# Weight-quarter sums by accumulating transfers, and another order of the seven products, in the up-projection of a decoder layer

## The chip, the cores and the metric

The kernel runs on one core of one Trainium2 chip. Its engines are TensorE (PE; its weight loads are listed apart, as PEld), VectorE (DVE), ScalarE (ACT), GpSimd (POOL) and SyncE (SP). SP and POOL do little here but issue transfers, each from a queue in which one transfer waits behind the one before it. The metric is the device time of one execution in microseconds (us), the median of several runs.

## The reference

One decoder layer on 576 tokens (512 of a prompt and 8 x 8 of samples), width 2048, everything in f32. Cut to the part that the change touches, the ConvFFN:

```python
up = rmsnorm(x, g_ffn) @ w_up                    # 2048 -> 2 * 5632
up_ext = jnp.concatenate([ffn_hist.astype(up.dtype), up], axis=1)
upc = causal_dwconv(up_ext, w_dw_f, b_dw_f)      # width 3
x = x + (jax.nn.silu(upc[..., :D_FF]) * upc[..., D_FF:]) @ w_down
```

Ahead of it stand the input projection, two head groups and the output projection; behind it a gate for a per-layer input and a last norm. Outputs are the activations and the new convolution states.

## The kernel before

**Phases.** All products of weights run one after the other on TensorE, as phases of one stream: mix (input projection), out and out2 (output projection), proj (per-layer input), **up**, down0 to down3, ple, tail. The tokens lie along the free axis as two halves of 288.

**Weights.** They come from DRAM as one stream, `in_wstream`, in the order in which they are used. A *unit* is 8 tiles of 128 x 128, 512 KB, and is loaded on SP's queue into a buffer `raw` (5 buffers, L189 in the function that loads a unit). Half a unit, 4 tiles, is a *piece*. To keep f32 accuracy each piece is split in two: ScalarE copies it to a rounded high half `wh` (L229) and VectorE subtracts that to get the low half `wl` (L230). Each has 4 buffers, so a piece can be split once TensorE has finished with the piece four before it. Activations are split in the same way, and a tile takes three matmuls: high by high, high by low, low by high (L695, L696, L697 in up).

**Up.** It computes 44 pairs `j` of column tiles: tile j and tile 44 + j of `w_up`, which the gate later multiplies. For a pair the weights are a 2 x 2 block of quarters (even and odd row tiles by the two column tiles), the tokens two halves, and one level of Strassen's scheme in Winograd's form takes 7 products of 8 tiles in place of 8. A product is 2 pieces, or 24 matmuls. The tile stream holds the four quarters of a pair as units u to u + 3: q11, q21, q22, q12. Products 1, 2 and 4 use q11, q12 and q22 as they are. The others use sums: product 7 q21 + q11, product 5 q21 + q22, product 6 that plus q11, product 3 that again plus q12, one after the other in two buffers `sum` of half a quarter each. VectorE makes these sums when a piece is prepared (L205, L209, L211). The activation side of each product, `sx`, was made before.

**Results of a product.** A product accumulates in one bank of a PSUM tile of two banks; there are three such tiles. The table `PRODS` sets the order of the products, and `banks` pairs them: in the order 1, 5, 6, 7, 4, 2, 3 the tiles hold (1, 5), (6, 7), (4, 2), and product 3 takes the bank of 6. The output tiles `ua` and `ub` are put together from the banks by one ScalarE copy after product 1 (L706) and VectorE operations after 6 (L709, L710), 7 (L713, L714), 4 (L716), 2 (L718) and 3 (L720). Waits between engines are kept by tile, not by bank: a matmul that begins in the second bank of a tile waits for readers of its first bank.

**Order of work.** A scheduler orders each engine's instructions; it moves a few matmuls of the next product but one ahead, where the next product has to wait. Half of the pairs write `ua` and `ub` to DRAM (L722, L723, POOL) and are fetched later, the other half go on at once to convolution and gate, whose result is written (`hidd`, L726, POOL). This work, and norm work in the first pairs, is dealt out between pieces as a queue `todo`. In the last pair the first fetches for the down phase are issued after products 1 and 6.

**At the start of up** the buffers `sum` of the first two pairs are those of two spare x rows and two spare activation tiles (`SPARE`, taken in turn by even and odd pairs). The proj phase just before it writes 16 results to DRAM from POOL (`pjd`, L885), and the scaled x rows are copied on ScalarE (`xg`, L565).

Of the kernel before, what the change touches and what calls it, by code (L numbers as in the profile page):

```python
# [11 lines left out]
ALU = mybir.AluOpType  # L12
PSUM = bass.MemoryType.PSUM

P = 128
# [4 lines left out]
HT = 288  # L20
# [6 lines left out]
NF = DFF // P  # L27
# [19 lines left out]
HGRP = 6  # L47


PRODS = [1, 5, 6, 7, 4, 2, 3]  # L50

VEC = {}
_n = 0
# [6 lines left out]
UNIT = 8  # L60
SUB = 4
# [66 lines left out]
def weight_order():  # L128

    tiles, pieces = [], []
    for phase, outs, ks in plan():
        n = len(tiles)
        if phase == "up":
            (w, a), (_, b) = outs
            for m, odd in ((a, 0), (b, 0), (b, 1), (a, 1)):
                tiles += [(w, k, m) for k in range(odd, KT, 2)]
            pieces += [(n // UNIT, prod, half) for prod in PRODS for half in range(2)]
        else:  # L140
            tiles += [(w, k, m) for k in ks for w, m in outs]
            for s in range(-(-n // SUB), -(-len(tiles) // SUB)):
                pieces.append((s * SUB // UNIT, s % 2))
    assert len(tiles) % UNIT == 0
    return tiles, pieces
# [3 lines left out]
def trunk_kernel(ctx: ExitStack, tc: tile.TileContext, A, O):  # L149
    nc = tc.nc  # L150
    groups = plan()
    order, pieces = weight_order()
    n_w = len(order)
# [5 lines left out]
    def tl(shape, tag, name, bufs=1, dt=F32):  # L159
        return pool.tile(shape, dt, tag=tag, name=name, bufs=bufs)  # L160

    def tmp(name, shape=(P, 2, HT)):
        return tl(list(shape), "t", name, bufs=6)


    raws, parts = {}, {}
# [7 lines left out]
    SPARE = [f"xh{LATE[2]}", f"xl{LATE[2]}", f"res{KT - 2}", f"res{KT - 1}"]  # L174
# [6 lines left out]
    def load_unit(u):  # L181
        if u in raws or u * UNIT >= n_w:
            return
        t = tl([P, UNIT * P], "raw", f"raw{u}", bufs=5)
        if u == 0:
            nc.sync.dma_start(t[:, : SUB * P], A["wstream"][u][:, : SUB * P])
            nc.sync.dma_start(t[:, SUB * P :], A["wstream"][u][:, SUB * P :])
        else:
            nc.sync.dma_start(t, A["wstream"][u])  # L189
        raws[u] = t  # L190

    sums = {}

    def source(p):

        if len(p) == 2:
            u, half = p
            return raws[u][:, half * SUB * P : (half + 1) * SUB * P]
        u, prod, half = p
        q11, q21, q22, q12 = (raws[u + n][:, half * SUB * P : (half + 1) * SUB * P] if u + n in raws else None  # L200
                              for n in range(4))
        if prod in (4, 1, 2):
            return {4: q22, 1: q11, 2: q12}[prod]
        if prod == 7:
            nc.vector.tensor_tensor(out=q21, in0=q21, in1=q11, op=ALU.add)  # L205
            return q21
        if prod == 5:
            sums[half] = tl([P, SUB * P], SPARE[2 * (u // 4 % 2) + half], f"sum{u}_{half}")
            nc.vector.tensor_tensor(out=sums[half], in0=q21, in1=q22, op=ALU.add)  # L209
        else:  # L210
            nc.vector.tensor_tensor(out=sums[half], in0=sums[half], in1=q11 if prod == 6 else q12, op=ALU.add)  # L211
        return sums[half]

    def prepare(s):
        if s in parts or s >= len(pieces):
            return
        p = pieces[s]
        u = p[0] if len(p) == 2 else p[0] + {1: 0, 5: 1, 6: 1, 7: 1, 4: 2, 2: 3, 3: 3}[p[1]]
        for a in range(4):
            load_unit(u + a)  # L220
        spare = s - (len(pieces) - 4)
        if spare < 0:
            h = tl([P, SUB * P], "wh", f"wh{s}", bufs=4, dt=F32R)
            l = tl([P, SUB * P], "wl", f"wl{s}", bufs=4, dt=F32R)
        else:
            h = tl([P, SUB * P], HID[32 + 2 * spare], f"wh{s}", dt=F32R)
            l = tl([P, SUB * P], HID[33 + 2 * spare], f"wl{s}", dt=F32R)
        src = source(p)
        nc.scalar.activation(h, src, AF.Copy)  # L229
        nc.vector.tensor_tensor(out=l, in0=src, in1=h.bitcast(F32), op=ALU.subtract)  # L230
        parts[s] = (h, l)

    at = {"tile": 0}

    def weights(i=None):

        n = at["tile"] if i is None else at["tile"] + i
        s = n // SUB
        for a in range(s, s + (4 if s >= 3 else 2)):
            prepare(a)  # L240
        if i is None:
            at["tile"] += 1
        h, l = parts[s]
        o = n % SUB * P
        return h[:, o : o + P], l[:, o : o + P]
# [117 lines left out]
    def deal():  # L363
        state["credit"] += state["rate"]
        if chain:
            take(chain)
        while (urgent or todo) and state["credit"] > 0:
            take(urgent or todo)
        if not (urgent or todo):
            state["credit"] = min(state["credit"], 0.0)  # L370
# [285 lines left out]
    def slot_of(j):  # L656
        return ORDER.index(j) % (len(HID) // 2)
# [8 lines left out]
    def fetch_hidden(j, slot):  # L666

        if j in hid_d:
            def fetch():
                p = tmp(f"hq{j}")  # L670
                nc.sync.dma_start(p, hid_d[j])
                split_hidden(j, slot, p)

            return [(0.7, fetch)]
        z = {}

        def fetch_up():
            for m, tag in ((j, "cv"), (NF + j, "vn")):
                z[m] = tl([P, 2, HT], tag, f"uz{m}", bufs=2)
                nc.sync.dma_start(z[m], up_d[m])  # L680

        return ([(0.0, fetch_up)] + conv_f(j, j, lambda: z[j]) + conv_f(j, NF + j, lambda: z[NF + j])
                + hidden(j, lambda p: split_hidden(j, slot, p)))

    banks = {}

    def up_pair(j):

        q = {}
        for n, prod in enumerate(PRODS):  # L690
            q[prod] = dst = banks[prod]
            for k in range(KT // 2):
                wh, wl = weights()
                bh, bl = sums_x[k][prod]
                nc.tensor.matmul(dst, wh, bh, start=k == 0, stop=False)  # L695
                nc.tensor.matmul(dst, wh, bl, start=False, stop=False)  # L696
                nc.tensor.matmul(dst, wl, bh, start=False, stop=k == KT // 2 - 1)  # L697
                if k % SUB == SUB - 1:
                    deal()
            if j == NF - 1 and prod in (1, 6):  # L700
                for i in ORDER[: 4] if prod == 1 else ORDER[4 : COMING[0]]:
                    for _, f in fetch_hidden(i, slot_of(i)):
                        f()
            if prod == 1:
                a = tl([P, 2, HT], "cv", f"ua{j}", bufs=2)
                nc.scalar.activation(a[:, 0, :], q[1], AF.Copy)  # L706
            if prod == 6:
                u = tl([P, HT], "q", f"uu{j}", bufs=2)
                nc.vector.tensor_tensor(out=u, in0=q[6], in1=a[:, 0, :], op=ALU.subtract)  # L709
                nc.vector.tensor_tensor(out=a[:, 1, :], in0=q[5], in1=u, op=ALU.add)  # L710
            if prod == 7:
                b = tl([P, 2, HT], "vn", f"ub{j}", bufs=2)
                nc.vector.tensor_tensor(out=u, in0=u, in1=q[7], op=ALU.subtract)  # L713
                nc.vector.tensor_tensor(out=b[:, 1, :], in0=q[5], in1=u, op=ALU.add)  # L714
            if prod == 4:
                nc.vector.tensor_tensor(out=b[:, 0, :], in0=u, in1=q[4], op=ALU.subtract)  # L716
            if prod == 2:
                nc.vector.tensor_tensor(out=a[:, 0, :], in0=q[2], in1=a[:, 0, :], op=ALU.add)  # L718
            if prod == 3:
                nc.vector.tensor_tensor(out=a[:, 1, :], in0=q[3], in1=a[:, 1, :], op=ALU.subtract)  # L720
        if j in up_d:
            nc.gpsimd.dma_start(up_d[j], a)  # L722
            nc.gpsimd.dma_start(up_d[NF + j], b)  # L723
            return
        todo.extend(conv_f(j, j, lambda: a) + conv_f(j, NF + j, lambda: b)
                    + hidden(j, lambda p: nc.gpsimd.dma_start(hid_d[j], p)))  # L726
# [23 lines left out]
    for gi, (phase, outs, ks) in enumerate(groups):  # L750
# [21 lines left out]
        if phase == "up" and prev != "up":  # L772
            settle(lambda: not todo)
            state["credit"], state["rate"] = 0.0, 0.36
            acc6 = [psum.tile([P, 2, 512], F32, tag="acc", name=f"acc_up{n}", bufs=3) for n in range(3)]
            banks.update({p: acc6[n // 2][:, n % 2, :HT] for n, p in enumerate((1, 5, 6, 7, 4, 2))})
            banks[3] = banks[6]
            rows_of(ORDER[0])
        if phase == "down0" and prev == "up":
            settle(lambda: not todo)  # L780
# [18 lines left out]
        if phase == "up":  # L799
            j = outs[0][1]  # L800
# [56 lines left out]
        for n, (w, m) in enumerate(outs):  # L857
# [24 lines left out]
            elif w == "w_ple_proj":  # L882
                a = tmp(f"pa{m}")
# [159 lines left out]
```

## Time and profile before

| what | us |
|---|---|
| median of 3 runs (lowest to highest) | 2480.53 (2479.83 to 2482.52) |
| profiled execution, its own time | 2480.28 |
| its span in the trace | 2478.3 |
| TensorE busy | 2449.2 |
| VectorE busy | 1841.9 |
| ScalarE busy | 1093.3 |
| POOL busy | 92.1 |
| DMA, mean over the span | 119 GB/s |
| the phase up in the trace | 677 to 1696 |

The span is what the trace shows from the first to the last instruction; the time of an execution has some 2 us around it. "Busy" for TensorE counts any time in which a matmul is in flight, so it doesn't tell how closely the matmuls follow each other. In the group lists a row gives line, engine, operation, output <- inputs, shapes and count; behind the first bar the busy time and the mean duration of one in ns; behind the second the idle time of the engine just before such instructions and what ended most of it. In the timeline a row begins with start and duration. In the table by stretches the columns are named where it is shown.

### The profile page before, as it was taken

To read this page: it belongs to the slowest core of one execution; us is meant where nothing else is said; L and a number is where in the kernel's file an instruction comes from. 1 tells how busy PE (TensorE), PEld (TensorE's weight loads), DVE (VectorE), ACT (ScalarE), POOL (GpSimd) and SP (SyncE) were. 2 spreads that over 40 slices of the span, in tenths; PEclk is the share of its full clock that TensorE was granted. 3 is DMA by queue.
4 is the path that set the end of the run, shared out by engine and by line. 5 is a ranking of instruction groups with operands and counts; after the bars stand their busy time and mean duration, and the time that the engine had idled before them with its cause. 6 is when DMAs were issued, how large, how long until landed. Compare 5 with 4: busy or idle time off the path is not lost.

```text
span 2478.3 us, 45398 instructions
## 1 busy us (share of the span) xinstructions
PE 2449.2 (99%) x18200; PEld 2418.2 (98%) x18200; DVE 1841.9 (74%) x3243; ACT 1093.3 (44%) x2028; POOL 92.1 (4%) x175
## 2 busy tenths in 40 slices
PE   9999999999999999999999999999999999999997
PEld 9999999999989999999999999999999999999997
DVE  7877788885998888888988888887549762254545
ACT  6444445433754444444544444445335441243334
POOL 1000000000200000000000000000000000000000
PEclk9999999999999999999999999999999999999998
DMA  6332222332653333333333333348425442222332
GB/s 235 94 83 83 84 88 85 127 107 95 227 184 111 109 115 110 110 126 106 102 123 113 102 118 118 97 152 281 127 89 154 136 126 78 85 86 80 116 100 95
DMA packets 106195, 294.70 MB, mean 119 GB/s; under 512 B 23568, under 2 KB 27792, under 8 KB 105984
## 3 DMA queue, kind: packets, MB, share of 16 engines
q1 hardware_dynamic: 96096, 259.20, 33.5%
q0 software_dynamic: 9744, 32.60, 3.6%
q8 instruction: 142, 2.33, 0.4%
q14 instruction: 69, 0.57, 0.1%
q10 hardware_dynamic: 144, 0.01, 0.0%
HBM read 255.43 MB, written 36.32 MB: 118 GB/s over the span
## 4 chain that ended last, share of the span: by engine, by line
PE 88%; issue 8%; DVE 2%; DMA 1%; ACT 1%; POOL 0%; DVEq 0%; ACTq 0%; SPq 0%; POOLq 0%
PE acc L835 18%; PE acc L839 18%; PE acc L837 18%; PE acc_up L695 10%; PE acc_up L697 10%; PE acc_up L696 10%; DVE wl L230 1%; DMA raw<-in_wstream 0%; PE vps L492 0%; PE mps L530 0%; ACT wh L229 0%; DVE y L945 0%; PE acc L908 0%; PE acc L909 0%; PE acc L910 0%
## 5 line engine op out<-in xcount | busy, mean ns | idle before, releaser
L229 ACT ACTIVATE wh<-raw 128x512 fp32r<-128x512 f32 x792 | 497.3, 632 | 1051.4 <-PE acc L837 670.5
L230 DVE TENSOR_TENSOR wl<-raw,wh 128x512 fp32r<-128x512 f32 x792 | 540.8, 688 | 390.9 <-ACT wh L229 383.3
L695 PE MATMUL acc_up<-sx,wh 128*128 128x288 f32 x2464 | 734.3, 299 | 2.5 <-ACT wh L229 1.2
L697 PE MATMUL acc_up<-sx,wl 128*128 128x288 f32 x2464 | 722.0, 298 | 5.5 <-DVE wl L230 5.1
L696 PE MATMUL acc_up<-sx,wh 128*128 128x288 f32 x2464 | 726.8, 295 | 0.0
L695 PEld LDWEIGHTS acc_up<-sx,wh 128*128 128x128 f32 x2464 | 464.0, 188 | 14.0 <-ACT ua L706 4.7
L697 PEld LDWEIGHTS acc_up<-sx,wl 128*128 128x128 f32 x2464 | 460.5, 188 | 17.5 <-DVE wl L230 17.1
L696 PEld LDWEIGHTS acc_up<-sx,wh 128*128 128x128 f32 x2464 | 464.0, 188 | 0.1
L835 PE MATMUL acc<-xh,wh 128*128 128x288 f32 x1984 | 427.4, 296 | 5.5 <-ACT wh L229 5.3
L839 PE MATMUL acc<-xh,wl 128*128 128x288 f32 x1984 | 423.9, 295 | 0.0
L837 PE MATMUL acc<-xl,wh 128*128 128x288 f32 x1984 | 423.8, 295 | 0.0
L835 PEld LDWEIGHTS acc<-xh,wh 128*128 128x128 f32 x1984 | 318.8, 189 | 7.5 <-ACT wh L229 5.3
L837 PEld LDWEIGHTS acc<-xl,wh 128*128 128x128 f32 x1984 | 319.5, 188 | 0.3 <-issue 0.2
L839 PEld LDWEIGHTS acc<-xh,wl 128*128 128x128 f32 x1984 | 318.4, 188 | 0.3 <-issue 0.3
L839 PE MATMUL acc<-hh,wl 128*128 128x288 f32 x1408 | 300.9, 295 | 0.0
L835 PE MATMUL acc<-hh,wh 128*128 128x288 f32 x1408 | 300.4, 294 | 0.4 <-ACT wh L229 0.4
L837 PE MATMUL acc<-hl,wh 128*128 128x288 f32 x1408 | 300.4, 295 | 0.0
L229 ACT ACTIVATE wh<-sum 128x512 fp32r<-128x512 f32 x264 | 166.5, 631 | 153.2 <-PE acc_up L696 137.3
L835 PEld LDWEIGHTS acc<-hh,wh 128*128 128x128 f32 x1408 | 226.2, 188 | 0.9 <-ACT wh L229 0.6
L837 PEld LDWEIGHTS acc<-hl,wh 128*128 128x128 f32 x1408 | 226.0, 188 | 0.0
L839 PEld LDWEIGHTS acc<-hh,wl 128*128 128x128 f32 x1408 | 225.7, 188 | 0.0
L230 DVE TENSOR_TENSOR wl<-sum,wh 128x512 fp32r<-128x512 f32 x264 | 180.5, 684 | 4.4 <-ACT wh L229 4.0
(191 smaller groups left out, 2146.5 us busy)
## 6 DMA issues: line engine op xcount, KB each, us to landing
raw<-in_wstream SPq DMA_DIRECT2D x395, 512.0 KB
uz<-upd SPq DMA_DIRECT2D x44, 288.0 KB
upd<-ub POOLq DMA_DIRECT2D x22, 288.0 KB, 2.8
upd<-ua POOLq DMA_DIRECT2D x22, 288.0 KB, 2.4
hidd<-hp POOLq DMA_DIRECT2D x22, 288.0 KB, 2.4
hq<-hidd SPq DMA_DIRECT2D x22, 288.0 KB
x<-in_xT SPq DMA_DIRECT2D x16, 288.0 KB
xr<-in_xT SPq DMA_DIRECT2D x16, 288.0 KB
```

Of the source, the lines that this page charges most:

```text
L229: nc.scalar.activation(h, src, AF.Copy)
L230: nc.vector.tensor_tensor(out=l, in0=src, in1=h.bitcast(F32), op=ALU.subtract)
L695: nc.tensor.matmul(dst, wh, bh, start=k == 0, stop=False)
L696: nc.tensor.matmul(dst, wh, bl, start=False, stop=False)
L697: nc.tensor.matmul(dst, wl, bh, start=False, stop=k == KT // 2 - 1)
L835: nc.tensor.matmul(accs[n][:, h, :HT], wh, bh[:, h, :], start=st, stop=False)
L837: nc.tensor.matmul(accs[n][:, h, :HT], wh, bl[:, h, :], start=False, stop=False)
L839: nc.tensor.matmul(accs[n][:, h, :HT], wl, bh[:, h, :], start=False, stop=sp)
```

## The change

The order of the products becomes 5, 7, 1, 6, 4, 2, 3, and the tiles of PSUM hold (5, 7), (1, 6), (4, 2), with product 3 in the bank of 1. The quarters of a pair lie in the stream as q21, q11, q22, q12. VectorE no longer adds weights. When the first unit of a pair is loaded, a new function issues: an accumulating transfer from DRAM onto that raw buffer (q21 + q11, for product 7); for each half, a plain copy of q21 into a `sum` buffer on SP and an accumulating transfer of q22 onto it (for product 5). Once the split of a piece of product 5 has read the sum, an accumulating transfer adds q11 to it, for 6; after 6 another adds q12, for 3. All accumulating transfers are issued by POOL. A pair so has 7 of them and two more plain copies. The function that loads ahead now looks four units ahead from the unit in use. The four VectorE operations that used to be shared between products 6 and 7 all stand behind 6.

```diff
-PRODS = [1, 5, 6, 7, 4, 2, 3]
+PRODS = [5, 7, 1, 6, 4, 2, 3]
...
-            for m, odd in ((a, 0), (b, 0), (b, 1), (a, 1)):
+            for m, odd in ((b, 0), (a, 0), (b, 1), (a, 1)):
...
-        if prod == 7:
-            nc.vector.tensor_tensor(out=q21, in0=q21, in1=q11, op=ALU.add)
-            return q21
-        if prod == 5:
-            sums[half] = tl([P, SUB * P], SPARE[2 * (u // 4 % 2) + half], f"sum{u}_{half}")
-            nc.vector.tensor_tensor(out=sums[half], in0=q21, in1=q22, op=ALU.add)
-        else:
-            nc.vector.tensor_tensor(out=sums[half], in0=sums[half], in1=q11 if prod == 6 else q12, op=ALU.add)
-        return sums[half]
+    def half_of(u, half):
+        return A["wstream"][u][:, half * SUB * P : (half + 1) * SUB * P]
+
+    def load_sums(u):
+
+        nc.gpsimd.dma_start(raws[u], A["wstream"][u + 1], accum_op=ALU.add)
+        for half in range(2):
+            t = sums[u, half] = tl([P, SUB * P], SPARE[2 * (u // 4 % 2) + half], f"sum{u}_{half}")
+            nc.sync.dma_start(t, half_of(u, half))
+            nc.gpsimd.dma_start(t, half_of(u + 2, half), accum_op=ALU.add)
+
+    def load_to(u):
+        for a in range(u, u + 4):
+            if a not in raws and a * UNIT < n_w:
+                load_unit(a)
+                if 0 <= a - first_up < n_up and (a - first_up) % 4 == 0:
+                    load_sums(a)
...
-        u = p[0] if len(p) == 2 else p[0] + {1: 0, 5: 1, 6: 1, 7: 1, 4: 2, 2: 3, 3: 3}[p[1]]
-        for a in range(4):
-            load_unit(u + a)
+        if len(p) == 2:
+            load_to(p[0])
+            src = raws[p[0]][:, p[1] * SUB * P : (p[1] + 1) * SUB * P]
+        else:
+            u, prod, half = p
+            n = {5: 0, 7: 0, 1: 1, 6: 1, 4: 2, 2: 3, 3: 3}[prod]
+            load_to(u + n)
+            src = sums[u, half] if prod in (5, 6, 3) else raws[u + n][:, half * SUB * P : (half + 1) * SUB * P]
...
+        if len(p) == 3 and p[1] in (5, 6):
+            nc.gpsimd.dma_start(src, half_of(u + (1 if prod == 5 else 3), half), accum_op=ALU.add)
...
             if prod == 6:
+                b = tl([P, 2, HT], "vn", f"ub{j}", bufs=2)
                 u = tl([P, HT], "q", f"uu{j}", bufs=2)
                 nc.vector.tensor_tensor(out=u, in0=q[6], in1=a[:, 0, :], op=ALU.subtract)
                 nc.vector.tensor_tensor(out=a[:, 1, :], in0=q[5], in1=u, op=ALU.add)
-            if prod == 7:
-                b = tl([P, 2, HT], "vn", f"ub{j}", bufs=2)
                 nc.vector.tensor_tensor(out=u, in0=u, in1=q[7], op=ALU.subtract)
                 nc.vector.tensor_tensor(out=b[:, 1, :], in0=q[5], in1=u, op=ALU.add)
...
-            banks.update({p: acc6[n // 2][:, n % 2, :HT] for n, p in enumerate((1, 5, 6, 7, 4, 2))})
-            banks[3] = banks[6]
+            banks.update({p: acc6[n // 2][:, n % 2, :HT] for n, p in enumerate((5, 7, 1, 6, 4, 2))})
+            banks[3] = banks[1]
```

In the changed kernel the three matmul lines of up are L702, L703 and L704, the copy after product 1 is L713, the writes of `ua`, `ub` and `hidd` L728, L729 and L732, `pjd` L891; the new transfers are L202 (onto `raw`), L205 (plain copies), L206 (q22 onto `sum`) and L238 (q11 or q12 onto `sum`).

**TensorE inside a pair.** First the kernel before, where product 1 (`sx_2`, tile 7931) ends and product 5 (`sx_3`, second bank of the same tile) is held; the rows between are of product 6 (tile 7932):

```order
L697 MATMUL acc_up_7931<-sx_2_7875,wl_12489 128x288
L695 MATMUL acc_up_7932<-sx_3_7146,wh_12545 128x288 [waits DVE_49,Activation_49]
L696 MATMUL acc_up_7932<-sx_4_7147,wh_12545 128x288
L697 MATMUL acc_up_7932<-sx_3_7146,wl_12546 128x288 [waits DVE_49]
L695 MATMUL acc_up_7932<-sx_3_7271,wh_12545 128x288
L695 MATMUL acc_up_7931<-sx_3_7146,wh_12506 128x288 [waits Activation_49]
L696 MATMUL acc_up_7931<-sx_4_7147,wh_12506 128x288
```

Now the changed kernel, in the order of time: product 5 (tile 7936) goes over to product 7 (`sx_0`, the same tile), and later product 1 (tile 7937) is followed by rows of product 4 (tile 7938) ahead of product 6.

```order
L704 MATMUL acc_up_7936<-sx_3_7885,wl_11979 128x288
L702 MATMUL acc_up_7936<-sx_0_7143,wh_11995 128x288 [waits Activation_49]
L703 MATMUL acc_up_7936<-sx_1_7144,wh_11995 128x288
L704 MATMUL acc_up_7937<-sx_2_7884,wl_12056 128x288
L702 MATMUL acc_up_7938<-sx_0_7143,wh_12107 128x288 [waits Activation_49]
L703 MATMUL acc_up_7938<-sx_1_7144,wh_12107 128x288
L704 MATMUL acc_up_7938<-sx_0_7143,wl_12108 128x288 [waits DVE_49]
L702 MATMUL acc_up_7937<-sx_3_7146,wh_12071 128x288 [waits Activation_49]
```

Between 5 and 7 there are no rows of another product, and the wait of the first row of 7 is that for its own piece; 6 behind 1 stands as 5 behind 1 did, with rows of 4 between instead of rows of 6. Counted over a whole pair, the rows went 1 (24), 6 (8), 5 (24), 6 (16), 4 (6), 7 (24), 4 (18), 3 (9), 2 (24), 3 (15) before, and go 5 and 7 (48), 1 (24), 4 (7), 6 (24), 4 (17), 3 (11), 2 (24), 3 (13) now.

**POOL at the start of up.** Before, the last writes of the proj phase (`pjd`) are followed by the first writes of `ua` and `ub`:

```order
L885 DMA pjd_157<-pa_7884 128x576
L885 DMA pjd_158<-pa_7908 128x576
L885 DMA pjd_159<-pa_7928 128x576
L723 DMA upd_183<-ub_8105 128x576
L722 DMA upd_182<-ua_7982 128x576
```

Now the accumulating transfers of the first pair stand among them (`sum_0` and `sum_1` are the two halves, the row of 128x1024 that of the second pair's raw buffer):

```order
L202 DMA raw_7963<-in_wstream 128x1024 [waits DMAHW5_49,DMAHW0_49,DMAHW6_49,DMASW6_49,DVE_49]
L891 DMA pjd_155<-pa_7835 128x576 [waits DMASW7_49,Activation_49]
L891 DMA pjd_156<-pa_7856 128x576 [waits DMASW0_49,Activation_49]
L206 DMA sum_0_7501<-in_wstream 128x512 [waits DMAHW1_49,DMASW1_49,Activation_49]
L891 DMA pjd_157<-pa_7893 128x576 [waits DMASW2_49,Activation_49]
L206 DMA sum_1_7504<-in_wstream 128x512 [waits DMAHW2_49,DMASW3_49]
L891 DMA pjd_158<-pa_7913 128x576 [waits DMASW4_49,Activation_49]
L891 DMA pjd_159<-pa_7933 128x576 [waits DMASW5_49,Activation_49]
L238 DMA sum_0_7501<-in_wstream 128x512 [waits DMASW6_49,DMASW1_49,DVE_49]
```

The first matmul of up was of product 1, from a plain load, and is now of product 5, from these sums.

**POOL in a steady pair.** Before, the queue holds nothing but three writes for two pairs, here with a neighbour on each side:

```order
L722 DMA upd_198<-ua_11756 128x576 [waits DMASW0_49,DVE_49]
L726 DMA hidd_166<-hp_12483 128x576 [waits DMASW1_49,DVE_49]
L723 DMA upd_201<-ub_12409 128x576 [waits DMASW2_49,DVE_49]
L722 DMA upd_200<-ua_12290 128x576 [waits DMASW3_49,DVE_49]
L726 DMA hidd_167<-hp_13016 128x576 [waits DMASW4_49,DVE_49]
```

Now, for the pair of `sum` 12295 and 12298 and the next one (12568, 12571):

```order
L729 DMA upd_201<-ub_12432 128x576 [waits DMASW4_49,DVE_49]
L202 DMA raw_12565<-in_wstream 128x1024 [waits DMAHW7_49,DMAHW0_49,Activation_49]
L238 DMA sum_0_12295<-in_wstream 128x512 [waits DMASW6_49,DVE_49]
L206 DMA sum_0_12568<-in_wstream 128x512 [waits DMAHW0_49,DMASW7_49,DMASW1_49]
L206 DMA sum_1_12571<-in_wstream 128x512 [waits DMAHW1_49,DMASW2_49]
L238 DMA sum_1_12298<-in_wstream 128x512 [waits DVE_49]
L728 DMA upd_200<-ua_12396 128x576 [waits DVE_49]
L238 DMA sum_0_12295<-in_wstream 128x512 [waits DMASW6_49,DMASW3_49,DVE_49]
L238 DMA sum_1_12298<-in_wstream 128x512 [waits DMASW4_49,DMASW1_49,DVE_49]
```

The queue now holds seven accumulating transfers a pair between the same writes; the sums of the next pair are issued while those of this pair are still in use.

More of the change, by code (lines that the diff above doesn't have):

```diff
@@ L192, in trunk_kernel @@
     sums = {}
[L194 to L203, printed above, removed]
-        if prod == 7:
-            nc.vector.tensor_tensor(out=q21, in0=q21, in1=q11, op=ALU.add)
-            return q21
-        if prod == 5:
-            sums[half] = tl([P, SUB * P], SPARE[2 * (u // 4 % 2) + half], f"sum{u}_{half}")
-            nc.vector.tensor_tensor(out=sums[half], in0=q21, in1=q22, op=ALU.add)
-        else:
-            nc.vector.tensor_tensor(out=sums[half], in0=sums[half], in1=q11 if prod == 6 else q12, op=ALU.add)
-        return sums[half]
+    first_up = min(p[0] for p in pieces if len(p) == 3)
+    n_up = 4 * NF
+    def half_of(u, half):
[12 more added lines that the diff above has]
+                    load_sums(a)
     def prepare(s):
@@ L227, in prepare @@
             l = tl([P, SUB * P], HID[33 + 2 * spare], f"wl{s}", dt=F32R)
-        src = source(p)
         nc.scalar.activation(h, src, AF.Copy)
```

## The prediction

> **What bounds the kernel now.** The first view is the page's list of engines with its chain of waits.
>
> ```profile
> span 2478.3 us, 45398 instructions
> PE 2449.2 (99%) x18200; PEld 2418.2 (98%) x18200; DVE 1841.9 (74%) x3243; ACT 1093.3 (44%) x2028; POOL 92.1 (4%) x175
> PE 88%; issue 8%; DVE 2%; DMA 1%; ACT 1%; POOL 0%; DVEq 0%; ACTq 0%; SPq 0%; POOLq 0%
> ```
>
> TensorE is busy 99% of the span and holds 88% of the chain; VectorE, which the change relieves, holds 2%. A busy TensorE need not be dense, so the second view counts matmuls in stretches of time: the up phase, the down phase behind it, the middle of up, and four shorter pieces at the ends of up.
>
> ```profile
> 677.00:1696.00 1019.00, 1011.09 (x7399) 987.36 (x7398) 867.15 (x1517) 473.21 (x887) 38.77 (x74) 1.00 0.38 122
> 1696.00:2256.00 560.00, 559.57 (x4226) 559.15 (x4225) 328.17 (x531) 216.38 (x445) 3.60 (x9) 1.00 0.39 123
> 750.00:1650.00 900.00, 899.07 (x6602) 879.20 (x6601) 762.42 (x1342) 409.46 (x776) 32.90 (x63) 1.00 0.35 112
> 677.00:700.00 23.00, 21.31 (x156) 20.49 (x155) 22.04 (x38) 14.35 (x25) 2.07 (x4) 1.00 0.76 259
> 700.00:723.00 23.00, 22.81 (x168) 22.10 (x167) 20.27 (x35) 12.43 (x21) 1.09 (x2) 1.00 0.56 182
> 723.00:746.00 23.00, 19.90 (x143) 19.00 (x142) 20.57 (x32) 11.11 (x20) 0.54 (x1) 1.00 0.33 108
> 1675.00:1696.00 21.00, 19.09 (x126) 18.14 (x125) 16.29 (x27) 11.06 (x21) 0.00 (x0) 0.92 0.74 232
> ```
>
> The columns are the stretch, its length, the busy time and count of PE, PEld, DVE, ACT and POOL, the granted clock, the DMA share and GB/s. In the down phase a matmul takes 560/4226 = 0.1325 us; that is TensorE undisturbed. The 7399 of up would take 980.4 us so and take 1019, so **up loses 38.6 us**, and this is all that a change in up can win. In the middle, 6602 would take 874.8 of 900 us: 25.2 us lost. One pair of column tiles is 7 products of 24 matmuls, 168 x 900/6602 = 22.9 us, so 39.3 pairs lie in this window and each loses 0.64 us. A piece of 12 matmuls undisturbed is 1.59 us, a product 3.18 us.
>
> Who is waited for is read from the groups of that window, weight loads only, and from the timeline.
>
> ```profile
> L695 PEld LDWEIGHTS acc_up<-sx,wh 128*128 128x128 f32 x2201 | 414.1, 188 | 10.1 <-ACT ua L706 4.7
> L697 PEld LDWEIGHTS acc_up<-sx,wl 128*128 128x128 f32 x2200 | 410.5, 188 | 10.7 <-DVE wl L230 10.5
> 894.07 0.19 PEld L695 LDWEIGHTS acc_up<-sx,wh 128*128 128x128 f32 x1 [0.24 <-ACT ua L706]
> ```
>
> The loads idle 20.8 us of the 900. Of the 10.1 us ahead of a first matmul (L695) the largest part, 4.7, ends with the copy `ua` that empties a product's bank; the 10.7 ahead of a third one (L697) end with the low half `wl` of a piece. The order of the matmuls says where: before, three products of a pair go into the second bank of a tile whose first bank has still to be read (5 after 1, 7 after 6, 2 after 4). TensorE fills each hold with a few matmuls of the product after, whose `wl` may not be ready yet. These **three holds** are the 0.64 us.
>
> **The change part by part.**
>
> *The VectorE sums go.* Their three groups:
>
> ```profile
> L211 DVE TENSOR_TENSOR sum<-sum,raw 128x512 f32<-128x512 f32 x176 | 120.7, 689 | 3.5
> L209 DVE TENSOR_TENSOR sum<-raw,raw 128x512 f32<-128x512 f32 x88 | 60.2, 686 | 21.8 <-DMA raw<-in_wstream 21.7
> L205 DVE TENSOR_TENSOR raw<-raw,raw 128x512 f32<-128x512 f32 x88 | 58.4, 683 | 0.0
> ```
>
> That is 352 instructions and 239.3 us of VectorE. I cost this at nothing by itself: VectorE is busy 762 of 900 us in the window, has room, and the path is TensorE. Where it could show is the `wl` waits, at most 10.5 us in the window; that is a rival below.
>
> *The accumulating transfers come.* Per pair: 7 on the POOL queue (one of 512 KB, six of 256 KB, 2.10 MB) and two plain copies of 256 KB on the SP queue (0.52 MB). The trace before holds no accumulating transfer, so its price is unknown. What the engines can carry is read from a dense stretch:
>
> ```profile
> 1704.00:1710.00 6.00, 6.00 (x48) 6.00 (x47) 2.46 (x4) 1.88 (x3) 0.54 (x1) 1.00 1.04 408
> ```
>
> The DMA engines are full (share 1.04) at 408 GB/s, 9.34 MB in 22.9 us. A pair now moves 112 GB/s x 22.9 us = 2.57 MB; with the copies 3.09. If an accumulated byte costs x copied ones, the load is 3.09 + 2.10x MB: 56% for x = 1, 78% for x = 2, full at **x = 3.0**. The lower bound is x = 1, as no accumulated byte can cost less than a copied one; above there is no bound in the trace. I take a value under 3: nothing is added to the sum, and past 3 each tenth costs 0.21 MB/408 GB/s x 44 = 22.6 us. The Trainium skill, "Collectives: The Full Stack", section "The bandwidth ceiling: the fold count and why AG ≠ RS ≠ AR", says that a reducing transfer reads two sources over the same ring and so runs at half the rate of a copy, and that the add costs nothing (62.28 against 32.35 GB/s, 1.93 times). No run here shows it; by it a pair would load the engines to 76%, an estimate from that page, and the sum would stand as it is.
>
> Beside the rate there is the delay. The nearest rows:
>
> ```profile
> upd<-ub POOLq DMA_DIRECT2D x22, 288.0 KB, 2.8
> upd<-ua POOLq DMA_DIRECT2D x22, 288.0 KB, 2.4
> x1d<-x POOLq DMA_DIRECT2D x16, 288.0 KB, 3.4
> es<-in_histA POOLq DMA_DIRECT2D x8, 120.0 KB, 4.6
> out_conv_a_sample<-es POOLq DMA_DIRECT2D x8, 120.0 KB, 6.5
> L726 POOL DMA_DIRECT2D hidd<-hp x22 | 11.9, 543 | 682.6 <-DVE hp L647 682.6
> L230 DVE TENSOR_TENSOR wl<-sum,wh 128x512 fp32r<-128x512 f32 x264 | 180.5, 684 | 4.4 <-ACT wh L229 4.0
> L229 ACT ACTIVATE wh<-sum 128x512 fp32r<-128x512 f32 x264 | 166.5, 631 | 153.2 <-PE acc_up L696 137.3
> ```
>
> A POOL transfer takes 0.54 us to issue and 2.4 to 6.5 us to land. The tightest is the accumulate onto the sum of product 6, needed by product 3. A piece can be split when TensorE ends the piece four before it, 3 x 1.59 = 4.8 us ahead of its turn; copy and subtract take 0.63 + 0.68, so the accumulate starts 3.5 us before product 6 does. TensorE starts product 3 as the filler about two products later (6.4 us), and its own split takes 1.3: 3.5 + 6.4 - 1.3 = **8.6 us** for issue and landing, against 2.9 to 7.0. It fits. POOL issues 7 x 0.54 = 3.8 us a pair; behind a waiting accumulate stand only the writes of `ua` and `ub`, which nobody waits for until the last pairs, and other accumulates. Behind a waiting copy of a sum on SP stand the next weight loads. Behind a `wh` that waits for a late sum stand ScalarE's evictions.
>
> *The order of products and banks.* 5 and 7 share a tile, and no reader comes between them; 6 is held by 1, and 2 by 4. Three holds become two. Steady pairs: 40 x 0.64/3 = **-8.6 us**. The four reads now crowd behind product 6, so the hold at 2 may grow: bounds 0 (the two left grow by what the third was) and -17 (two of three gone).
>
> *The start of up.* Product 1 needed a plain load; now product 5 is first and needs the accumulated sum.
>
> ```profile
> 673.08 1.47 ACT L565 ACTIVATE xg<-x,vec 128x576 f32<-128x576 f32 x2
> 677.03 0.29 PE L695 MATMUL acc_up<-sx,wh 128*128 128x288 f32 x1
> ```
>
> The two buffers that the first sums take are those of x rows 14 and 15, whose last reader is this pair of copies; the first of them ends half way, at 673.8. Then a plain copy (2.4 to 3.4 us by the rows of 288 KB above), an accumulate (0.54 + 2.4 to 4.6) and the ScalarE copy (0.63): 679.8 to 683.0, middle 681.4, instead of 677.0: +2.8 to +6.0, taken **+4.4 us**. Idle time of this length has a second price:
>
> ```profile
> 1682.00:1684.00 2.00, 0.91 (x6) 0.68 (x6) 1.45 (x4) 1.15 (x4) 0.00 (x0) 0.98 0.40 154
> 1684.00:1686.00 2.00, 2.00 (x11) 2.00 (x10) 2.00 (x4) 0.57 (x2) 0.00 (x0) 0.50 0.01 4
> 1686.00:1688.00 2.00, 2.00 (x12) 2.00 (x12) 1.46 (x3) 0.61 (x1) 0.00 (x0) 0.66 0.31 33
> ```
>
> After 1.1 us without matmuls the granted clock was 0.50, then 0.66: 2 x 0.50 + 2 x 0.34 = **+1.7 us** once. Against it, the first pair loses 23 - 156 x 0.1325 = 2.3 us to work that is late; that work runs on during the stall: **-2.3**. The next two lose 0.7 and 4.1; a third of the first and some of the second: **-1**.
>
> *The last pair.* 1675 to 1696 loses 21 - 126 x 0.1325 = 4.3 us: a burst of fetches of hidden rows, that now comes behind the third and fourth product. A hold less: **-1.4** (bounds -4 and +3, as the two bursts stand closer).
>
> Sum: -8.6 + 4.4 + 1.7 - 2.3 - 1.0 - 1.4 = -7.2. The profiled execution took 2480.28 us, span 2478.3 and 2.0 around it, 0.25 below the median 2480.53 (2479.83 to 2482.52). So **2473 us**, 0.3% faster. About 0.2%, 5 us, is what a measurement here can tell from no change.
>
> **The rivals.**
>
> *The accumulates are too dear (slower).* In up's steady pairs: from x = 3 the DMA engines set the pace. At x = 3.3, 3.09 + 6.93 = 10.0 MB take 24.6 us instead of 22.9: +1.7 x 44 = +75, less 7: **2548**. For it: nothing shows x, and the engines are already at 35%. Against: a byte read and written twice is x = 2, and there is a third of the capacity to spare even so. A landing delay beyond 8.6 us has the same place and sign with a smaller price: each us over is one us a pair, 44 us. 30%.
>
> *No change within 0.2%.* The stall at the start is at its upper end (+6.0 + 1.7) and the two holds left take what the third gave, half of the 8.6: 2480.3 - 4.3 + 7.7 - 2.3 - 1 - 1.4 = **2479**. For it: the VectorE work behind product 6 is four instructions in a row ahead of the reader of product 4. 22%.
>
> *The lighter VectorE also ends the `wl` waits.* The filler behind product 1 is now of product 4, which needs no sum; half of the 10.5 us in the window and half of the rest of a hold go too: 2473 - 10 = **2463**. For it: that 10.5. Against: a filler is late because it is pulled forward, not because VectorE is full. 10%.
>
> **How the numbers follow.** My forecast 38%, dear accumulates 30%, no change 22%, `wl` waits gone 10%. Faster by over 0.2% (under 2475.5): the 10% and most of the forecast, 0.46; within: 0.24; slower: 0.30. The range goes from 2458 (steady pairs at -17, the rest as summed, and a little of the `wl` waits) to 2570, x = 3.4: past that I leave out about 1 in 10, below 2458 less than 1 in 10. The forecast's own range is 2465 to 2480.
>
> **What would show it.** The holds: in the middle of up, matmuls per 900 us should rise from 6602 to about 6665 (25.2 lost to 16.8). If 7 still waits for a reader of 5, the bank argument is wrong. The start: first matmul of up near 681, ended by a copy from `sum`, and a row with the clock near 0.5 behind it; if near 677, the term of +6.1 is wrong. The transfers: DMA share in the middle 0.55 to 0.80 and waits for `sum` or `raw` from POOL's queue near none; a share near 1.00 and TensorE idle before `wh<-sum` means that x is 3 or more. The prediction is wrong if the weight loads in up wait mostly for DMA.

## The result, and the profile after

The changed kernel takes 2666.68 us in the median (2663.55 to 2668.03), the kernel before beside it 2481.53. The ratio is 1.0745, 95% interval 1.0726 to 1.0763: **slower by 7.5%**, 185 us. The range on record ended at 2570.

The page of the changed kernel begins so, with the same columns as before:

```profile
span 2665.7 us, 45745 instructions
PE 2504.1 (94%) x18200; PEld 2473.4 (93%) x18200; DVE 1638.5 (61%) x2891; ACT 1096.9 (41%) x2028; POOL 359.4 (13%) x483
PE 30%; DVE 1%; DMA 0%; issue 0%; ACT 0%; DVEq 0%; ACTq 0%
```

TensorE has the same 18200 matmuls and is busy a smaller share; VectorE has lost what it was to lose. The chain of waits breaks off after 31% of the span, so it isn't used. The table by stretches tells more: the start of up, its middle, and three short pieces of the middle, 40 us or one and a half pairs of column tiles in all.

```profile
660.00:750.00 90.00, 71.84 (x482) 69.63 (x481) 47.30 (x80) 44.99 (x76) 25.07 (x35) 0.89 0.86 242
750.00:1650.00 900.00, 802.68 (x5595) 785.94 (x5594) 494.68 (x872) 351.33 (x659) 229.41 (x286) 0.94 0.79 193
1016.00:1029.00 13.00, 13.00 (x100) 12.88 (x98) 8.37 (x15) 6.31 (x14) 5.16 (x6) 1.00 0.98 220
1029.00:1040.00 11.00, 9.20 (x67) 8.85 (x67) 8.89 (x16) 5.54 (x11) 1.99 (x3) 1.00 0.69 181
1040.00:1056.00 16.00, 13.75 (x104) 13.51 (x103) 5.66 (x10) 4.54 (x8) 5.76 (x7) 1.00 1.01 246
```

In the middle 5595 matmuls run in 900 us instead of 6602. Undisturbed (0.1325 us each) they need 741 us, so 159 are lost, and with a pair now 168 x 900/5595 = 27.0 us long that is 4.8 us a pair instead of 0.64. Over 40 pairs this is 165 us more, most of the 187 by which the span grew. The kernel before runs 615 matmuls between 660 and 750, this one 482: 133 x 0.1325 = 17.6 us more. The DMA share of the middle is 0.79, but it is not even: in turn 0.98, 0.69 and 1.01.

The weight loads of that window, and who ended their waits:

```profile
L702 PEld LDWEIGHTS acc_up<-sx,wh 128*128 128x128 f32 x1863 | 368.3, 199 | 96.3 <-ACT wh L234 95.3 <-ACT ua L713 0.9
L704 PEld LDWEIGHTS acc_up<-sx,wl 128*128 128x128 f32 x1863 | 365.6, 197 | 17.6 <-DVE wl L235 17.6
```

TensorE waits for ScalarE's split copy, `wh`; of the 159 us lost, 114 are idle time of these loads. ScalarE, in the list of waits of the whole run (us in total, times, longest), waits for a sum, and the issues by size and time to landing name the transfer:

```profile
ACT wh L234 <- DMA sum<-in_wstream: 197.4, 54, 6.4
sum<-in_wstream POOLq DMA_DIRECT2D x264, 256.0 KB, 6.9
raw<-in_wstream POOLq DMA_DIRECT2D x44, 512.0 KB, 5.5
```

One pair shows how. The timeline of POOL, then of ScalarE (start, duration, engine, line):

```profile
1041.03 0.88 POOL L202 DMA_DIRECT2D raw<-in_wstream  x1 [1.16 <-DMA sum<-in_wstream]
1042.00 0.86 POOL L238 DMA_DIRECT2D sum<-in_wstream  x1
1042.56 2.04 POOL L206 DMA_DIRECT2D sum<-in_wstream  x2
1043.89 1.58 POOL L238 DMA_DIRECT2D sum<-in_wstream  x1
...
1055.26 0.63 ACT L234 ACTIVATE wh<-sum 128x512 fp32r<-128x512 f32 x1 [5.36 <-DMA sum<-in_wstream]
```

POOL issues five accumulating transfers within 3 us. Three are not read before the next pair (L202, L206 twice); two are wanted now (L238: q11 onto the halves of product 5's sum, which makes the sum of 6). The second of them is issued last, at 1043.89, and the split that reads it starts at 1055.26, **11.4 us later**, after 5.4 us of waiting.

The other 45 us are matmuls that ran slower. The granted clock, third column from the end, is 0.94 in the middle and was 1.00 before. Two rows around the stall of this pair show where it is lost:

```profile
1054.00:1056.00 2.00, 0.00 (x0) 0.00 (x0) 0.08 (x1) 0.74 (x2) 0.00 (x0) 1.00 0.96 233
1058.00:1060.00 2.00, 2.00 (x10) 2.00 (x10) 0.00 (x0) 0.00 (x0) 0.00 (x0) 0.50 0.76 96
```

Behind a stretch without a matmul the clock was 0.50. Between 750 and 1650 the trace has 24 such slow stretches, 102 us in all, and none in the kernel before. At half clock they are worth up to 51 us, so **some 30% of the loss is the clock** that falls behind the stalls.

### The profile page after: what moved, and what is told of

Its sections match the earlier page's. It is cut to its first block, busy times and chain, and to the rows that moved or that the text cites. A ratio compares the mean times of both kernels' runs of the same rounds, so it can differ in the third digit from the quotient of the medians.

```text
span 2665.7 us, 45745 instructions
## 1 busy us (share of the span) xinstructions
PE 2504.1 (94%) x18200; PEld 2473.4 (93%) x18200; DVE 1638.5 (61%) x2891; ACT 1096.9 (41%) x2028; POOL 359.4 (13%) x483
## 3 DMA queue, kind: packets, MB, share of 16 engines
q0 software_dynamic: 54096, 124.89, 23.6%
## 5 line engine op out<-in xcount | busy, mean ns | idle before, releaser
L702 PE MATMUL acc_up<-sx,wh 128*128 128x288 f32 x2464 | 752.9, 309 | 121.5 <-ACT wh L234 118.6
L704 PE MATMUL acc_up<-sx,wl 128*128 128x288 f32 x2464 | 749.2, 307 | 15.2 <-DVE wl L235 14.9
L703 PE MATMUL acc_up<-sx,wh 128*128 128x288 f32 x2464 | 749.2, 305 | 0.0
L702 PEld LDWEIGHTS acc_up<-sx,wh 128*128 128x128 f32 x2464 | 488.0, 199 | 133.1 <-ACT wh L234 129.2
L704 PEld LDWEIGHTS acc_up<-sx,wl 128*128 128x128 f32 x2464 | 484.8, 198 | 26.7 <-DVE wl L235 26.6
L703 PEld LDWEIGHTS acc_up<-sx,wh 128*128 128x128 f32 x2464 | 487.5, 198 | 0.1
L238 POOL DMA_DIRECT2D sum<-in_wstream x176 | 173.5, 987 | 415.4 <-DVE wl L235 301.8
## 6 DMA issues: line engine op xcount, KB each, us to landing
upd<-ua POOLq DMA_DIRECT2D x22, 288.0 KB, 11.4
```

Of the source, the lines that this page charges most:

```text
L238: nc.gpsimd.dma_start(src, half_of(u + (1 if prod == 5 else 3), half), accum_op=ALU.add)
```

## The experiments

All stand against runs of the kernel before on the same chip.

| label | median us | ratio, 95% interval |
|---|---|---|
| e1_vector_sums | 2469.27 | 0.9958 (0.9944 to 0.9973) |
| e2_urgent_first | 2491.67 | 1.0055 (1.0038 to 1.0072) |
| e3_plain | 2480.75 | 1.0006 (0.9996 to 1.0015) |
| e4_hybrid | 2485.24 | 1.0020 (1.0011 to 1.0030) |
| e5_no_filler | 2658.09 | 1.0733 (1.0701 to 1.0764) |
| e6_no_holds | 2445.33 | 0.9861 (0.9847 to 0.9874) |
| e7_order_and_start | 2480.90 | 1.0005 (0.9996 to 1.0014) |
| e8_start_alone | 2653.13 | 1.0701 (1.0685 to 1.0718) |
| e9_later_start | 2470.32 | 0.9961 (0.9948 to 0.9973) |
| e11_all | 2449.45 | 0.9876 (0.9861 to 0.9891) |

**Is it the transfers or the order of products?** e1 keeps order, units and tiles of the change and makes all sums on VectorE.

```diff
-                    load_sums(a)
...
+            if prod == 5:
+                nc.vector.tensor_tensor(out=sums[u, half], in0=q21, in1=q22, op=ALU.add)
+            if prod == 7:
+                nc.vector.tensor_tensor(out=q21, in0=q21, in1=q11, op=ALU.add)
+            if prod in (6, 3):
+                nc.vector.tensor_tensor(out=sums[u, half], in0=sums[u, half], in1=q11 if prod == 6 else q12, op=ALU.add)
...
-            nc.gpsimd.dma_start(src, half_of(u + (1 if prod == 5 else 3), half), accum_op=ALU.add)
```

> The new order of products, units and banks, with all sums made on VectorE again and no accumulating transfer. Theory A (the late accumulating transfers are the whole loss): 2465 to 2475 us, since two holds a pair are left of three and product 5, now first, needs only plain loads. Rival B (the new order of products itself costs something): clearly over 2485.

2469.27, as expected. The order of products is worth 11 us of gain, and all of the loss, 197 us against this run, is the transfers'. Its middle of up:

```profile
750.00:1650.00 900.00, 899.06 (x6693) 890.10 (x6692) 771.62 (x1365) 426.97 (x788) 33.33 (x64) 1.00 0.36 115
```

6693 matmuls instead of 6602: 12.1 us won in the window, with VectorE as busy as before. What is left is 900 - 6693 x 0.1325 = 13.2 us, 0.33 a pair.

**Order in the queue, load, or delay?** From the second pair on, e2 issues the same transfers with the two urgent ones first (`issue_after` keeps what its block issues behind the named instruction on that queue).

```diff
-        nc.gpsimd.dma_start(raws[u], A["wstream"][u + 1], accum_op=ALU.add)
...
+            d = nc.gpsimd.dma_start(src, half_of(u + (1 if prod == 5 else 3), half), accum_op=ALU.add)
+            if half:
+                with tc.issue_after(d.ins):
+                    if prod == 5:
+                        at["a5"] = d
+                    else:
+                        while late_raw:
+                            add_raw(late_raw.pop(0))
+        if len(p) == 3 and "a5" in at:
+            with tc.issue_after(at["a5"].ins):
+                while late:
+                    a = late.pop(0)
+                    for half in range(2):
+                        add_sums(a, half)
```

> The same transfers as the changed kernel, but on POOL's queue the two that are needed soon (q11 onto the sum of product 5) stand ahead of those for the next pair: the q22 ones come behind them, the one onto the raw buffer behind those for product 6. Theory A1 (a burst of transfers that have time stands ahead of the urgent ones): 2485 to 2510, what is left being mostly the start of up. Rival A2 (the DMA engines can't carry the accumulating load in any order): over 2620. Rival A3 (each accumulating transfer takes 7 us or more to land, whatever stands before it): about 2600.

2491.67: 175 of the 185 us are back with not a byte less. POOL's timeline and the middle of up in this run:

```profile
1017.73 0.84 POOL L252 DMA_DIRECT2D sum<-in_wstream  x1 [11.03 <-DVE wl L249]
1019.28 0.84 POOL L252 DMA_DIRECT2D sum<-in_wstream  x1 [0.71 <-DVE wl L249]
1019.82 2.04 POOL L204 DMA_DIRECT2D sum<-in_wstream  x2
...
750.00:1650.00 900.00, 899.11 (x6698) 890.48 (x6697) 592.47 (x1041) 425.23 (x784) 273.72 (x342) 1.00 0.93 230
```

The two urgent transfers (here L252) go out before the two of the next pair (L204). The DMA share has *risen* to 0.93, since the pairs are shorter, and TensorE runs 6698 matmuls at a clock of 1.00. So the load can be carried. Taken apart from the two traces by their place in the pair, between 900 and 1650, the second urgent transfer lands in 10.5 us (median; 8.6 to 12.1, 28 of them) in the changed kernel and in 4.4 (3.9 to 6.3, 33) here. Here, where it is in time, the split that reads it comes 6.8 us behind its issue; for the second transfer onto the sum of product 3 that time is 8.0.

**What is a transfer's place made of?** e3 leaves the queue's order as the change has it and makes every accumulating transfer a plain copy, so the sums of weights are left out.

```diff
-        nc.gpsimd.dma_start(raws[u], A["wstream"][u + 1], accum_op=ALU.add)
+        nc.gpsimd.dma_start(raws[u], A["wstream"][u + 1])
```

> The accumulating transfers become plain copies of the same bytes on the same queue in the same order, so the sums of weights are left out. By the packets an accumulated 2 KB takes 178 ns of an engine and a copied one 84. Theory A1 (burst of engine time): the burst halves, 2480 to 2510. A2: the same. Rival A3 (a fixed landing time of POOL's transfers): 2600 or more, as before.

2480.75: with the same five transfers in the same order, the stall is gone, and POOL's transfers onto `sum` land in 4.2 us instead of 6.9. The second urgent one, still the last of five, lands in 5.3 (4.0 to 8.0, 33 of them) instead of 10.5. So the place in the queue costs little when those ahead are cheap. What costs is that they accumulate: their time on the DMA engines, and their longer issue on POOL (0.84 us or more against 0.54 here), which no run separates. Waiting for its turn on POOL is the small part: in the changed kernel the second urgent transfer is issued 0.6 us (median, at most 2.0) after the split that it waits for. The software queue (number, kind, packets, MB, share of 16 engines' span), of the changed kernel:

```profile
q0 software_dynamic: 54096, 124.89, 23.6%
```

and of e3:

```profile
q0 software_dynamic: 37200, 124.89, 15.4%
```

The queue held 3.6% of 2478.3 = 89 us before. The change adds 23.6% of 2665.7 - 89 = 540 us, the plain copies 15.4% of 2482.9 - 89 = 293: **an accumulated byte costs 1.84 copied ones**. Packet by packet the medians are 178 ns against 84 for 2 KB, 2.1 times, so the ratio is about 2 and depends on how it is counted. The Trainium skill, "Collectives: The Full Stack", section "The bandwidth ceiling: the fold count and why AG ≠ RS ≠ AR", gives 1.93 for its reducing transfer and the second source read as the cause; 1.84 lies 5% below it and 2.1 above it, and the cause no run here shows.

**Only the urgent ones?** e4 keeps the three transfers a pair that have time and makes the sums for 6 and 3 on VectorE.

```diff
+            if prod in (6, 3):
+                nc.vector.tensor_tensor(out=sums[u, half], in0=sums[u, half], op=ALU.add,
+                                        in1=raws[u + n][:, half * SUB * P : (half + 1) * SUB * P])
...
-            nc.gpsimd.dma_start(src, half_of(u + (1 if prod == 5 else 3), half), accum_op=ALU.add)
```

> The three transfers a pair that have a whole pair's time stay accumulating (q11 onto raw, q22 onto both sums); the four urgent ones (for products 6 and 3) are VectorE additions again, 176 in all. Theory A1: no TensorE wait for a sum in the middle of up, 2480 to 2495 with the late start left. Rival A2: by 48% fewer accumulated bytes, still over 2500. Rival A3: as A1, as these have the time.

2485.24, in the range. Its middle runs 6699 matmuls in 900 us, as e2's; what it loses against e1 lies before 750 (510 matmuls between 660 and 750, against 633 in e1).

**Does the filler make a late sum dearer?** e5 forbids TensorE to run matmuls of product 4 ahead of product 6.

```diff
+                if prod == 4 and k == 0:
+                    tc.keep_in_program_order(first)
```

> The changed kernel, but the matmuls of product 4 stay behind all of product 6 on TensorE, so that nothing fills the hold ahead of 6. Theory F (the filler makes the late sum dearer: its pieces are split behind the second piece of product 6 on ScalarE, so TensorE waits for that piece before it has begun 6): 2540 to 2610 us, some 2 us less of a stall in each of 44 pairs. Rival (the stall is the lateness of the sum alone, wherever TensorE waits for it): 2660 or more.

2658.09: **the theory failed**, hardly 9 us came back. The list of waits of this run in the middle of up and three rows of ScalarE show why:

```profile
ACT wh L234 <- DMA sum<-in_wstream: 144.1, 56, 5.2
PEld acc_up L702 <- ACT ua L715: 105.5, 34, 5.3
```

```profile
1007.08 0.63 ACT L234 ACTIVATE wh<-sum 128x512 fp32r<-128x512 f32 x1 [3.95 <-DMA sum<-in_wstream]
1007.62 1.14 ACT L234 ACTIVATE wh<-raw 128x512 fp32r<-128x512 f32 x2
1008.66 0.39 ACT L715 ACTIVATE ua<-acc_up 128x288 f32<-128x288 f32 x1
```

Without the filler TensorE waits for `ua`, the copy that empties product 1's bank and so lets product 6 begin. ScalarE works in order, and this copy stands behind the `wh` that waits for the sum, as the splits of product 4 do. Either way product 6 can't begin until its *second* piece has been split. That a copy moved off that queue would win the time was not tried.

**The start.** e7 is e2 with the first two pairs' sums on VectorE, e8 is the changed kernel with the same, e9 is e7 with four pairs.

```diff
-                if 0 <= a - first_up < n_up and (a - first_up) % 4 == 0:
+                if 8 <= a - first_up < n_up and (a - first_up) % 4 == 0:
...
+            if u < first_up + 8:
```

> The changed kernel with the sums of the first two pairs on VectorE and its queue order as it was. Theory S: 2640 to 2655, the start being worth 12 to 25 us and nothing else altered. Rival (the late start also puts the later pairs out of step): under 2600.

> The kernel with the urgent transfers first, and the sums of the first two pairs made on VectorE, so that no accumulating transfer runs before the third pair. Theory S (what that kernel lost against sums on VectorE is all at the start: the wait for the first sum, and writes of the phase before that stand behind transfers on POOL's queue): 2466 to 2474. Rival (the load of the DMA engines costs it in steady pairs too): 2483 to 2492.

> As the kernel with urgent transfers first and the first two pairs on VectorE, but with the first four pairs on VectorE, so that accumulating transfers begin only when the 16 x rows of the norm have been fetched. Theory N (in pairs 1 and 2 the x rows come late beside the accumulating transfers, and ScalarE, which squares them, holds up the splits queued behind): 2466 to 2473 us, the same as with all sums on VectorE. Rival (each start of accumulating transfers costs about 10 us, wherever it lies): 2478 to 2484.

e8 took 2653.13, the start being worth 13.6 us, as expected. e7 took 2480.90, **between the theory and its rival**: 10.8 us back instead of some 20. The wait that was left lay in pairs 1 and 2; the list of waits between 695 and 755 of e7, and the stretch 660 to 750 of e2, e7 and e9:

```profile
ACT sq L324 <- DMA xs<-x1d: 16.1, 6, 4.6
```

```profile
660.00:750.00 90.00, 71.46 (x481) 68.43 (x480) 49.15 (x84) 47.20 (x82) 26.16 (x37) 0.91 0.88 241
```

```profile
660.00:750.00 90.00, 78.32 (x539) 75.73 (x538) 63.64 (x106) 50.91 (x88) 17.97 (x27) 0.93 0.74 222
```

```profile
660.00:750.00 90.00, 85.24 (x626) 83.16 (x625) 78.75 (x132) 56.29 (x97) 10.98 (x20) 1.00 0.60 201
```

In these pairs 16 rows of x are fetched for the norm and squared on ScalarE. Beside the accumulating transfers they land late, ScalarE stands at the square, and the splits behind it are late: the same engine, held by another transfer. With transfers from the fifth pair on, 2470.32: the start is whole again (626 matmuls against 481, and 3.7 us at the square instead of 16.1), and the kernel is about 1 us from e1.

**The holds.** e6 is the kernel before, sums on VectorE, in an order in which no product begins beside a bank that was finished just before it and still has to be read; e11 is e9 with such an order, 5, 1, 7, 6, 4, 3, 2. The edit of e6:

```diff
-PRODS = [1, 5, 6, 7, 4, 2, 3]
+PRODS = [1, 5, 7, 6, 4, 3, 2]
...
-            banks.update({p: acc6[n // 2][:, n % 2, :HT] for n, p in enumerate((1, 5, 6, 7, 4, 2))})
-            banks[3] = banks[6]
+            banks.update({p: acc6[n // 2][:, n % 2, :HT] for n, p in enumerate((5, 7, 1, 6, 4, 2))})
+            banks[3] = banks[1]
```

> Not the change, but what its order of banks points to: the kernel before with all sums on VectorE, the order 1, 5, 7, 6, 4, 3, 2 and the tiles (5, 7), (1, 6), (4, 2), 3 in the bank of 1. No product begins in a tile whose other bank was finished just before it and has readers. Theory H (the holds by tile are what a steady pair still loses): 2455 to 2463. Rival (two holds or none, the rest is something else): 2467 to 2472, as with two holds.

> The kernel of the run with later start, with the order of products 5, 1, 7, 6, 4, 3, 2 in the same tiles, so that no product begins in a tile whose other bank was finished just before. Theory H (holds by tile are the rest of the loss; sums by transfers in a good order cost steady pairs nothing): 2443 to 2452, as with VectorE sums in the order without holds. Rival (sums by transfers keep a cost that the two holds have hidden so far): 2455 or more.

2445.33 and 2449.45, **1.4 and 1.2% faster than the kernel before**. e6 won more than was expected: the start and the last pair gained too. It runs 661 matmuls between 660 and 750, 615 in the kernel before (6.1 us), and 152 in its last 21 us of up, 126 before (3.4 us). The middle of up, first of e6, then of e11:

```profile
750.00:1650.00 900.00, 900.00 (x6800) 900.00 (x6800) 787.06 (x1386) 435.87 (x805) 34.00 (x65) 1.00 0.38 120
```

```profile
750.00:1650.00 900.00, 900.00 (x6798) 900.00 (x6798) 606.54 (x1063) 429.92 (x800) 274.29 (x342) 1.00 0.96 234
```

6800 matmuls in 900 us are 0.1324 each: nothing is lost. The same speed comes with VectorE busy 787 us and the DMA engines 0.38, or VectorE 607 and the engines 0.96. Relieving VectorE is worth nothing here. Most of the 4 us between the two lies at the end of up, where the last matmul ends at 1660.9 in e6 and at 1664.5 in e11; why is not shown.

## Why the prediction was wrong, step by step

- **What bounds.** Right. Up lost 38.6 us, and e6, which takes the holds away, is faster by 34.
- **The VectorE sums at nothing.** Right: e6 makes all of them there and loses nothing in the middle.
- **The rate of the accumulating transfers.** Right that x is under 3: it is about 2. The room was smaller than the sum said. It set all bytes against 408 GB/s, while its own row, 112 GB/s at a share of 0.35, makes 320 GB/s at a full share; by that the engines would be full at x = 2.0, an estimate from this row. The load for x = 2, put at 78%, is 0.93 by the engines' share in e2.
- **The delay of their landing. This step failed**, in three places. It took the transfers for product 3 as the tightest, with 8.6 us; late were those for product 6, which in e2 have 6.8 us where those for product 3 have 8.0. (The 8.6 also counts 6.4 us from the start of product 6 to the filler of 3; by the rows counted with the change these are 41 matmuls, 5.4 us.) It sized the landing by plain transfers of a kernel without such bursts (2.4 to 6.5 us); within a burst the second urgent one took 10.5. And it said of POOL's queue that behind a waiting accumulate stand "other accumulates", without asking which of them is wanted first: the part on the change shows the two urgent rows (L238) behind one of 512 KB and, the second, behind two of 256 KB. An estimate was at hand: five transfers are 1.57 MB in 3 us, at the x = 2 that it named some 7.7 us of the engines at 408 GB/s, beside the weight loads.
- **What stands behind a late `wh`.** Named ("ScalarE's evictions"), and given no price. In e5 it ties TensorE to the late piece before its turn: the copy `ua` stands behind it.
- **The price of the clock.** Put once, at the start, at +1.7 us. There it came (0.50 between 690 and 694 us), but it came again behind the stalls of the middle: of the 4.1 us more that a pair lost, 2.9 are idle time of the weight loads and 1.2 slower matmuls.
- **The order of products.** Right in mechanism, mis-sized: -8.6 for 40 pairs, measured -12.1 for 39 (e1), inside its bounds. Two holds still cost 0.33 us a pair, none cost nothing (e6).
- **The start.** Mis-sized: net +2.8 against +17.6 us up to 750. The first matmul of up came at 689.6, not 681.4. The rows of the changed kernel, ScalarE and TensorE:

```profile
663.72 1.30 ACT L890 ACTIVATE pa<-acc 128x576 f32<-128x576 f32 x2 [4.68 <-DMA pjd<-pa]
682.44 1.19 ACT L890 ACTIVATE pa<-acc 128x576 f32<-128x576 f32 x2 [1.67 <-DMA pjd<-pa]
688.91 0.63 ACT L234 ACTIVATE wh<-sum 128x512 fp32r<-128x512 f32 x1 [4.17 <-DMA sum<-in_wstream]
689.60 0.61 PE L702 MATMUL acc_up<-sx,wh 128*128 128x288 f32 x1 [7.61 <-ACT wh L234]
```

  The wait for the sum was foreseen (4.4). Not foreseen was that the writes `pjd` on POOL's queue, moved behind accumulating transfers, give their buffers back late and so hold ScalarE and the phase before, 4.68 and 1.67 us; the order shown with the change has such rows mixed.
- **The last pair.** Of the wrong sign: -1.4 was forecast. The last 21 us of up, of e1 and of the changed kernel:

```profile
1663.80:1684.80 21.00, 15.61 (x101) 14.74 (x101) 15.47 (x26) 10.90 (x20) 0.00 (x0) 0.84 0.71 213
```

```profile
1862.40:1883.40 21.00, 14.83 (x92) 14.29 (x91) 13.90 (x24) 9.68 (x17) 0.00 (x0) 0.84 0.72 222
```

  101 matmuls against 126 before, with no accumulating transfer in the kernel: 3.3 us more from the order alone. About half of it, 1.7 us, is the granted clock (0.84 against 0.92); what brought it down further is not shown.
- **The rival.** "A landing delay beyond 8.6 us" had the place and the sign. Its price, 44 us for each us over, is too low from the 8.6 on: a landing of 10.5 is 1.9 over, 84 us, and 165 were lost. From the 6.8 us of e2 it is 3.7 over and 163; that this fits is in part luck, as the price has no term for the clock. The delay was put as the lesser part of the rival on the rate, which set the end of the range; it had no upper bound in the trace and should have set it.
- **The signs.** They could not tell this case. The DMA share of 0.79 lay in the band that was to confirm the forecast, and the idle time before `wh<-sum` was to mean x of 3 or more; x is about 2.

## What to carry to other kernels

When work moves from an engine to a queue, ask for each transfer when it is wanted, and read the queue's order: transfers with a whole pair's time stood ahead of one with some 7 us, and a new order of the same transfers gave back 175 of 185 us. Size a landing by the burst in which it stands (bytes ahead, at the engines' rate), not by the median of lone transfers; an average DMA share of 0.79 hid stretches at 1.0. Price the clock for every stall, not once: here it was some 30% of the loss. And an in-order engine that waits for a late transfer holds back all that stands behind it, evictions above all.

## What the runs showed that was not expected

- Issuing an accumulating transfer takes POOL longer, 0.84 us against 0.54 for the same transfer as a plain copy (e3), and 1.6 where issues follow closely (1043.89 above).
- DMA engines at a share of 0.93 to 0.96 over 900 us (e2, e11) cost TensorE nothing measurable when the transfers' order is right.
- Waits kept by tile of two banks were all that a steady pair lost: with the products in another order and other tiles, 0.64 us a pair became 0 (e6).
